# Differential attention: the fourth head through DRAM, norms by square transposes in tasks of their own, other banks for the values

## Chip, cores and metric

The kernel runs on one core of one Trainium2 chip. The metric is the device time of one execution in microseconds (us), the median of several runs. A core has a matrix engine (TensorE, PE), a vector engine (VectorE, DVE), a scalar engine (ScalarE, ACT), a general engine (GpSimd, POOL), a queue processor (SyncE, SP) and 16 DMA engines; each runs its own instruction stream in order and waits on semaphores.

## What is computed

One layer of a streaming encoder for 512 tokens of 1024 channels in float32: four mixers (A differential attention, B forgetting attention, C a convolution module, D a short gated convolution) fed by one input projection and merged by gates, then cross-attention into 256 memory tokens, then a gated MLP. The change touches branch A:

```python
s = einsum('bqhcd,bkhcd->bhcqk', q_blk, k) * scale          # 4 heads, 2 components c of 64 channels
mask = k_chunk[None, :] <= (tq_blk // CHUNK)[:, None]        # chunks of 64 tokens
p = softmax(where(mask, s, -inf), axis=-1)
a = p[:, :, 0] - lam * p[:, :, 1]
ya = einsum('bhqk,bkhe->bqhe', a, v)                         # e: 128 channels of a head
ya = rms_norm(ya, diff_norm) * (1 - lambda_init)             # over the 128 channels
```

## The kernel before

All matrix products are float32 work in reduced passes: an operand is split into a high part and a low remainder (ACT writes the high part, DVE subtracts it to get the low one), and three matmuls hi*hi, hi*lo, lo*hi are summed in a bank (`mm3`). Activations lie with channels on the partitions and tokens along the row (`ht`, high and low); weights stream in through SP, are split into `wh` and `wl`, and each block of weights is one job of `run_blocks`, which fetches three jobs ahead.

Beside the jobs runs a planner, `Background(0.7, 2)`. Attention heads and norms are Python generators ("tasks") that emit a few instructions at each step and yield a cost and a wait. A clock advances with every matmul and transpose emitted (0.00042 per column, 0.107 per turn); at each `tick`, after a job and in the middle of some, the first two tasks of the queue may take steps whose wait is over, as far as a credit of 0.7 per unit of clock allows. `drain(name)` steps the named tasks to their end without letting the clock decide. What is emitted is then ordered for each engine by a scheduler at build time, which works on its own estimates of durations and moves an instruction ahead of others when its inputs and buffers are free; `tc.issue_after` and `keep` restrict it. The order on each engine is fixed in the program.

`mixer_jobs` sets the order around the change: branch D's gates, A's value products, then for each of the four heads of A its query and key products (`qk_jobs`), which add `a_task`, and some of the twelve gate jobs of branch C (0, 2, 4, 6 after the four heads); then `drain("a")`, branch B's value products (`vf_jobs`; the code calls branch B "f" and its values "vf"), B's heads (`f_task`) beside branch A's gate jobs.

`a_task` for a head: for each of four blocks of 128 queries, scores of both components into two "sc" banks (the block sees 128, 256, 384 or 512 keys), mask and maximum by a DVE operation into an "e" tile, two exponentials on ACT, reciprocals, and the difference of the two scaled parts (line 943). The result has queries on the partitions, and the values need it with keys there. For heads 0 to 2 (`far`), this turn is done by DVE in squares of 32x32 (`turn_squares`, line 854), a store to DRAM (`put`, line 859) and a load that places the squares (`get`, line 866), then a split in place (lines 872 and 873), at steps of their own; 8 steps. For head 3 it is done by PE matmuls with an identity (`to_keys_major`, `transpose`, line 247); 6 steps. `values` multiplies by the head's values into one "av" bank for two blocks at a time; a copy (line 952) takes the bank to an e tile. The norm over the head's channels follows in the same task, for every head: four turns by the identity bring tokens to the partitions, ACT squares (line 958), DVE sums (line 960), POOL takes the power (line 286), DVE scales (line 962), four more turns bring the channels back, and a split writes `y["a"]` (lines 164 and 165).

Two resources matter. Of e tiles there are three (`bufs=3`), which blocks, copies and other tasks share. Of PSUM there are eight banks: two each of "mm", "av" and "sc", one "tr0" and one "tr1"; in this stage the gate and query products rotate over mm, mm, tr0, and turns use tr1. The values of A and of B each fill the one tile tagged "v" (`bufs=1`).

`vf_jobs` multiplies the tokens by B's value weights: first tokens blocks 0 and 1, each into an mm and an av bank (256 and 264 columns), then, after their evacuation (`done`), blocks 2 and 3 into mm and av again.

`over_channels` (line 877) is one matmul with a 128x128 matrix `across`, which adds up, for each of the 32 positions within a square, the four partition groups; the convolution's norm uses it with sums over 32x32 squares that `by_token` groups.

Of the kernel before, what the change touches and what calls it, by code (L numbers as in the profile page):

```python
# [25 lines left out]
P = 128  # L26
# [20 lines left out]
class Background:  # L47
# [7 lines left out]
        self.queue, self.rate, self.width = [], rate, width  # L55
        self.clock = self.last = self.credit = 0.0

    def add(self, gen, name):
        self.queue.append([name, gen, 0.0])

    def step(self, task):
        try:
# [7 lines left out]
    def tick(self):  # L70
        self.credit = min(self.credit + (self.clock - self.last) * self.rate, 4.0)
        self.last = self.clock
        for task in list(self.queue[:self.width]):
            while self.credit > 0 and task in self.queue and task[2] <= self.clock:
                self.credit -= self.step(task)

# [7 lines left out]
def hybrid_layer(ctx: ExitStack, tc: tile.TileContext, a: dict, out: bass.AP):  # L84
# [751 lines left out]
    def to_keys_major(e, n, pt, local):  # L836

        ps = bank("tr")
        for kt in range(n):
            transpose(ps[:, kt * P:(kt + 1) * P], e[:, kt * P:(kt + 1) * P])  # L840
        split(ps[:, :n * P].rearrange("p (t a i) -> p a t i", t=n, a=4), *(x[:, local, :, :n] for x in pt))
# [9 lines left out]
    def turn_squares(dst, src):  # L851
        if len(dst.shape) == 2:
            dst = dst.rearrange("p (b t i) -> p b t i", b=4, i=32)
        V.transpose(dst, src.rearrange("p (t j b) -> p b t j", b=4, j=32))
# [10 lines left out]
    def get(d, n, pt, local):  # L865
        SP.dma_start(part_of(pt[1], n, local).bitcast(F32), d.rearrange("(a j) (b x) -> (j b) a x", j=32, b=4))

    def split_in_place(n, pt, local):
        hi, lo = (part_of(x, n, local) for x in pt)
        raw = lo.bitcast(F32)  # L870
        with tc.issue_after(evacuations[0]):
            A.copy(hi, raw)
        V.tensor_tensor(lo, raw, hi.bitcast(F32), ALU.subtract)
# [21 lines left out]
    def pt_tiles():  # L895
        return tuple(m1p.tile([P, 2, 4, 4, 32], F32R, tag=n, name=n, bufs=2) for n in ("pth", "ptl"))
# [3 lines left out]

    def a_task(h, qk, v):
        es, pt, av = {}, None, None
        far = h < 3
        yield 0.0, 3.0
        for step in range(8 if far else 6):
            if step in ((5, 7) if far else (3, 5)):
                if av is None:
                    av = bank("av")
                vh, vl = (x[:, :, h * P:(h + 1) * P] for x in v[0])
                with tc.issue_after(steps_of[0]) if far else ExitStack():  # L910
                    values(av, lambda kt: ((vh[:, kt], 0), (vh[:, kt], 1), (vl[:, kt], 0)), pt,
                           step // 2 - (2 if far else 1))
            cost = 0.0
            if far:
                for qt in SPLITS.get(step, ()):
                    split_in_place(qt + 1, pt, qt % 2)
                    cost += 0.1 + 0.15 * qt
                for qt in GETS.get(step, ()):
                    if qt % 2 == 0:
                        pt = pt_tiles()  # L920
                    get(es.pop(qt)[:, 0], qt + 1, pt, qt % 2)
            elif 1 <= step <= 4:
                if step in (1, 3):
                    pt = pt_tiles()
                to_keys_major(es.pop(step - 1)[:, 0], step, pt, (step - 1) % 2)
                cost += 0.1 + 0.15 * step
            if step < 4:
                qt, w = step, (step + 1) * P
                e = es[qt] = e4()
                st = m1p.tile([P, 8], F32, tag="st8", name="st8", bufs=4)  # L930
                for c in range(2):
                    ps = bank("sc")
                    scores(ps, qk, c, qt * P, w)
                    V.tensor_tensor_reduce(e[:, c, :w], ps[:, :w], mask_a[:, S - w:], scale=-HD ** -0.5,
                                           scalar=3.0e38, op0=ALU.add, op1=ALU.min,
                                           accum_out=st[:, c:c + 1])
                for c in range(2):
                    A.activation(e[:, c, :w], e[:, c, :w], AF.Exp, bias=st[:, c:c + 1],
                                 scale=-1.0, accum_out=st[:, 4 + c:5 + c])
                V.reciprocal(st[:, 6:8], st[:, 4:6])  # L940
                V.tensor_scalar(st[:, 7:8], st[:, 7:8], lam, None, ALU.mult)
                A.activation(e[:, 1, :w], e[:, 1, :w], AF.Copy, scale=st[:, 7:8])
                V.scalar_tensor_tensor(e[:, 0, :w], e[:, 0, :w], st[:, 6:7], e[:, 1, :w], ALU.mult,
                                       ALU.subtract)
                cost += 0.6 + 0.0035 * w
                if far:
                    turn_squares(e[:, 1, :w], e[:, 0, :w])
                    es[qt] = put(e[:, 1:], w)
                    cost += 0.0015 * w
            if step == (7 if far else 5):  # L950
                e = e4()
                A.copy(e[:, 0], av)
            yield cost, (6.0 if step == 5 else 4.0) if far else 3.5

        ps = bank("tr")
        for t in range(NT):
            transpose(ps[:, t * P:(t + 1) * P], e[:, 0, t * P:(t + 1) * P])
        A.activation(e[:, 1], ps, AF.Square, scale=1.0 / math.sqrt(P))
        ms = m1p.tile([P, NT], F32, tag="ms4", name="ms4", bufs=2)
        V.tensor_reduce(ms, e[:, 1].rearrange("p (t c) -> p t c", t=NT), AX.X, ALU.add)  # L960
        r = rstd_of(m1p, [ms], NT)
        V.tensor_tensor(e[:, 0].rearrange("p (t c) -> p t c", t=NT),
                        ps.rearrange("p (t c) -> p t c", t=NT),
                        r.unsqueeze(2).to_broadcast([P, NT, P]), ALU.mult)
        yield 1.5, 3.5
        ps2 = bank("tr")
        for t in range(NT):
            transpose(ps2[:, t * P:(t + 1) * P], e[:, 0, t * P:(t + 1) * P])
        if "a" not in y:
            y["a"] = (y8b(), y8b())  # L970
        split(ps2, y["a"][0][:, h], y["a"][1][:, h], half["dn"])
        yield 0.6, 0.0


    crows = dram.tile([8, S], F32, name="crows")
# [2 lines left out]
    def vf_jobs(dst):  # L978

        ps, held = {}, []  # L980
        groups = ((0, 256), (256, 520))

        def products(kb, tokens):
            hi, lo = held[kb]
            for t in tokens:
                sl = slice(t * P, (t + 1) * P)
                for k in range(2):
                    kk = kb * 2 + k
                    for g, (c0, c1) in enumerate(groups):
                        mm3(ps[t, g][:, :c1 - c0], ht[0][:, kk, sl], ht[1][:, kk, sl], hi[:, k, c0:c1],  # L990
                            lo[:, k, c0:c1], kk == 0, kk == NK - 1)

        def done(t):
            for g in range(2):
                hs = slice(4 * g, 4 * g + 4)
                split(ps[t, g][:, :256].rearrange("p (h c) -> p h c", h=4), dst[0][:, t, hs, 0], dst[0][:, t, hs, 1])
            V.tensor_copy(dst[1][:, t], ps[t, 1][:, 256:264])

        for kb in range(4):
            def body(hi, lo, kb=kb):  # L1000
                held.append((hi, lo))
                if kb == 0:
                    dst.append(m1p.tile([P, NT, 8, 2, HD], F32R, tag="v", name="v"))
                    dst.append(small["fz_raw"].rearrange("p (t h) -> p t h", t=NT))
                    ps.update({(t, g): bank(("mm", "av")[g]) for t in range(2) for g in range(2)})
                products(kb, (0, 1))
                if kb < 3:
                    return
                done(0)
                done(1)  # L1010
                bg.tick()
                ps.update({(t, g): bank(("mm", "av")[g]) for t in range(2, 4) for g in range(2)})
                for b in range(4):
                    products(b, (2, 3))
                    bg.tick()
                done(2)
                done(3)
                forget_gates(dst[1])

            yield *cols(w_in, O_FV, BR + 8, kb * 2, 2), body  # L1020
# [181 lines left out]
    def mixer_jobs():  # L1202
# [20 lines left out]
        yield from vj  # L1223
        yield share("mm", "mm", "tr0")
        gc = gate_blocks(2, "c")
        for h, n in enumerate((0, 2, 4, 6)):
            yield from qk_jobs(O_AQ, O_AK, h, lambda qk, h=h: bg.add(a_task(h, qk, va), "a"))
            if n:
                yield then(lambda: bg.drain("conv"))
            for _ in range(n):  # L1230
                yield next(gc)
# [666 lines left out]
```

## Time and profile before

| | us |
|---|---|
| median of 3 runs (lowest to highest) | 1048.19 (1047.79 to 1048.29) |
| the profiled execution, its own time | 1047.26 |
| its span, first to last instruction | 1045.5 |
| busy TensorE / VectorE / ScalarE / GpSimd | 1035.8 / 809.6 / 510.6 / 143.3 |

All rows of the profile are from one execution. Times in it start at the first instruction. A row of a timeline reads: start, length, engine, line, operation, output tile <- input tiles, shapes, count, and in brackets the idle time before it with what ended it. "PE ps_mm" is a matmul that writes a bank tagged mm. Lengths of matmul records overlap, since matmuls are pipelined; the chain of work that ended last gives each piece the time that it adds. In the groups by line the columns are busy time and mean length, then the engine's idle time before the group and what ended it. A row of the waits names the waiting engine, tile and line, whom it waited for, the total, how often, and the longest.

### The profile page before, as it was taken

How to read it: one execution, taken by the hardware profiler on the slowest of the kernel's cores; microseconds unless marked ns; L12 is line 12 of the kernel's file. 1: busy time of each engine (PE TensorE's matmuls, PEld its weight loads, DVE VectorE, ACT ScalarE, POOL GpSimd, SP SyncE). 2: the span in 40 equal slices, each digit the busy share in tenths (PEclk: the TensorE clock that was granted, in tenths of full speed). 3: DMA queues.
4: the chain of work that ended last, by engine and by line, in shares of the span. 5: the costliest groups of instructions: out<-in, count | busy, mean ns of one | idle time of the engine just before them, and what ended most of it. 6: DMA issues, size and time to landing. Idle time of an engine off the chain costs nothing.

```text
span 1045.5 us, 14417 instructions
## 1 busy us (share of the span) xinstructions
PE 1035.8 (99%) x5235; PEld 880.7 (84%) x5235; DVE 809.6 (77%) x1241; ACT 510.6 (49%) x838; POOL 143.3 (14%) x239
## 2 busy tenths in 40 slices
PE   9999999999999999999999999999999999999997
PEld 8888888888888988888888899998888888888886
DVE  7999998677787367878577898777767777667786
ACT  5322222376565365666444566555343333445662
POOL 4001000100010123342101031121112111111001
PEclk9999999999999999999999999999999999999999
DMA  8954333334433246666338744135676676626662
GB/s 271 311 156 100 101 101 101 91 91 121 142 104 109 62 122 178 184 165 158 120 124 287 237 134 127 62 108 184 193 240 229 214 227 217 220 82 183 216 214 82
DMA packets 187453, 166.48 MB, mean 159 GB/s; under 512 B 20415, under 2 KB 159148, under 8 KB 187381
## 3 DMA queue, kind: packets, MB, share of 16 engines
q1 hardware_dynamic: 178339, 133.80, 43.1%
q10 hardware_dynamic: 6482, 23.21, 6.1%
q0 software_dynamic: 2560, 8.54, 2.7%
q8 instruction: 41, 0.67, 0.3%
q14 instruction: 31, 0.25, 0.1%
HBM read 140.74 MB, written 24.79 MB: 158 GB/s over the span
## 4 chain that ended last, share of the span: by engine, by line
PE 99%; DMA 0%; DVE 0%; issue 0%; POOL 0%; POOLq 0%; DVEq 0%; SPq 0%; ACT 0%; ACTq 0%
PE ps_mm L241 47%; PE ps_av L241 30%; PE ps_tr L241 11%; PE ps_sc L241 7%; PE ps_tr L247 2%; PE ps_mm L459 1%; PE ps_av L459 1%; DMA xs<-in_x 0%; PE ps_tr L443 0%; DVE o L1788 0%; PE ps_av L443 0%; DVE nt L438 0%; DVE ge L1183 0%; DVE nt L412 0%; POOL st_m L285 0%
## 5 line engine op out<-in xcount | busy, mean ns | idle before, releaser
L198 ACT CAST wh<-wr 128x1024 fp32r<-128x1024 f32 (+1 forms) x140 | 146.5, 1047 | 233.5 <-PE ps_mm L241 121.2
L199 DVE TENSOR_TENSOR wl<-wr,wh 128x1024 fp32r<-128x1024 f32 (+1 forms) x140 | 174.8, 1249 | 86.2 <-ACT wh L198 85.4
L241 PE MATMUL ps_mm<-hth,wh 128*128 128x512 f32 (+1 forms) x536 | 198.9, 378 | 0.0
L241 PE MATMUL ps_mm<-htl,wh 128*128 128x512 f32 (+1 forms) x536 | 198.3, 377 | 0.0
L241 PE MATMUL ps_mm<-hth,wl 128*128 128x512 f32 (+1 forms) x536 | 198.3, 377 | 0.0
L241 PE MATMUL ps_av<-hth,wh 128*128 128x512 f32 (+1 forms) x328 | 122.5, 374 | 0.0
L241 PE MATMUL ps_av<-htl,wh 128*128 128x512 f32 (+1 forms) x328 | 122.5, 373 | 0.0
L241 PE MATMUL ps_av<-hth,wl 128*128 128x512 f32 (+1 forms) x328 | 122.3, 373 | 0.0
L241 PEld LDWEIGHTS ps_mm<-hth,wl 128*128 128x128 f32 x536 | 99.0, 188 | 18.3
L241 PEld LDWEIGHTS ps_mm<-hth,wh 128*128 128x128 f32 x536 | 99.0, 188 | 17.9 <-ACT hth L161 0.3
L241 PEld LDWEIGHTS ps_mm<-htl,wh 128*128 128x128 f32 x536 | 98.9, 188 | 17.9
L694 DVE SCALAR_TENSOR_TENSOR y<-y,par,y 128x508 f32<-128x508 f32 (+29 forms) x120 | 82.5, 725 | 0.1
L241 PEld LDWEIGHTS ps_av<-hth,wh 128*128 128x128 f32 x328 | 61.6, 188 | 11.1 <-DVE e L1154 0.3
L241 PEld LDWEIGHTS ps_av<-htl,wh 128*128 128x128 f32 x328 | 61.6, 188 | 10.9
L241 PEld LDWEIGHTS ps_av<-hth,wl 128*128 128x128 f32 x328 | 61.6, 188 | 10.9
L1689 DVE TENSOR_TENSOR wl<-dw,wh 128x1024 fp32r<-128x1024 f32 x32 | 40.2, 1260 | 15.0 <-ACT wh L1688 14.7
L1688 ACT CAST wh<-dw 128x1024 fp32r<-128x1024 f32 x32 | 33.4, 1051 | 22.2 <-PE ps_mm L241 7.4
L1636 ACT ACTIVATE th<-c 128x512 f32<-128x512 f32 x22 | 13.9, 632 | 48.8 <-DVE c L621 48.8
L1123 POOL TENSOR_SCALAR fbias<-ck,cq 128x128 f32<-128x128 f32 (+3 forms) x32 | 23.4, 739 | 73.0 <-DVE st L1129 66.6
L621 DVE SCALAR_TENSOR_TENSOR c<-ps_mm,par,c 128x510 f32<-128x510 f32 (+1 forms) x44 | 32.7, 744 | 0.7
L241 PE MATMUL ps_tr<-hth,wh 128*128 128x512 f32 x80 | 31.8, 398 | 0.0
L241 PE MATMUL ps_tr<-htl,wh 128*128 128x512 f32 x80 | 31.6, 395 | 0.0
(503 smaller groups left out, 2227.9 us busy)
## 6 DMA issues: line engine op xcount, KB each, us to landing
wr<-in_w_up SPq DMA_DIRECT2D x44, 512.0 KB
wr<-in_w_in SPq DMA_DIRECT2D x38, 512.0 KB
wr<-in_w_gate SPq DMA_DIRECT2D x32, 512.0 KB
wp<-in_w_down ACTq DMA_DIRECT2D x22, 512.0 KB
sums<-wp ACTq DMA_DIRECT2D x22, 512.0 KB
dw<-sums SPq DMA_DIRECT2D x44, 256.0 KB
wr<-in_w_branch SPq DMA_DIRECT2D x16, 512.0 KB
wide<-in_w_out SPq DMA_DIRECT2D x12, 512.0 KB
```

What stands on the lines that cost most here:

```text
L198: last_weights[:] = [order(A.copy(hi, raw[:, :n])).ins, low.tensor_tensor(lo, raw[:, :n], hi.bitcast(F32), ALU.subtract).ins]
L199: low.tensor_tensor(lo, raw[:, :n], hi.bitcast(F32), ALU.subtract).ins]
L241: steps_of[:] = [PE.matmul(ps, lhs, rhs, start=start, stop=stop).ins]
L247: turns.append(PE.transpose(ps, x, ident[:n, :n]).ins)
L459: keep(PE.matmul(banks[c][:, :S // 2], w[p == 1][:, k, c * P:(c + 1) * P], ht[p == 2][:, i * 4 + k, :S // 2], start=(i, p, k) == (0, 0, 0) ...
L621: ins = V.scalar_tensor_tensor(dst[:, s:], src[:, :S - s], w(k), dst[:, s:], ALU.mult, ALU.add)
L694: ins = V.scalar_tensor_tensor(dst[:, s:], src[:, :S - s], pc("conv_dw", k * 4 + j), dst[:, s:], ALU.mult, ALU.add)
L1123: G.tensor_scalar(bias[:, :w], ck[j][:, :w], -1.0, cq[:, qt, head:head + 1], ALU.mult, ALU.add)
L1636: A.activation(th, c[:, 0], AF.Silu)
L1688: A.copy(hi, x)
L1689: V.tensor_tensor(lo, x, hi.bitcast(F32), ALU.subtract)
```

## The change

Head 3 now takes the same way as heads 0 to 2 (8 steps, through DRAM). The norm leaves `a_task` and becomes a task of its own, `head_norm`, which the planner puts at the head of its queue with a wait of 4.0 and steps beside the two others: tasks added with `beside` raise the number of tasks that a tick may step. The norm uses DVE's square transposes in place of turns by the identity: after one, sums over 32 of the channels lie along the row, `over_channels` adds the four partition groups, the power is taken for 16 columns, the scaled squares are turned back and split. No turn by the identity is left in branch A. The gate jobs of branch C are dealt out as 0, 2, 3, 7. `vf_jobs` uses mm and sc for blocks 0 and 1, and av, tr0, av, mm for blocks 2 and 3.

```diff
@@ class Background
+    def add(self, gen, name, beside=None):
+        if beside is None:
+            self.queue.append([name, gen, 0.0, 0])
+        else:
+            self.queue.insert(0, [name, gen, self.clock + beside, 1])
...
-        for task in list(self.queue[:self.width]):
+        for task in list(self.queue[:self.width + sum(t[3] for t in self.queue)]):
@@ a_task
-        far = h < 3
...
-        for step in range(8 if far else 6):
+        for step in range(8):
...
-                to_keys_major(es.pop(step - 1)[:, 0], step, pt, (step - 1) % 2)
...
+                turn_squares(e[:, 1, :w], e[:, 0, :w])
+                es[qt] = put(e[:, 1:], w)
...
+            yield cost, 6.0 if step == 5 else 4.0
+        bg.add(head_norm(h, e), "a", 4.0)
+
+    def head_norm(h, e):
+        V.transpose(e[:, 1], e[:, 0])
+        A.activation(e[:, 0], e[:, 1], AF.Square, scale=1.0 / math.sqrt(P))
+        ms = m1p.tile([P, S // 32], F32, tag="ms4", name="ms4")
+        V.tensor_reduce(ms, by_token(e[:, 0]), AX.X, ALU.add)
+        yield 1.0, 4.0
         ps = bank("tr")
-        for t in range(NT):
-            transpose(ps[:, t * P:(t + 1) * P], e[:, 0, t * P:(t + 1) * P])
...
+        over_channels(ps[:, :S // 32], ms)
+        V.tensor_scalar(ms, ps[:, :S // 32], EPS, None, ALU.add)
+        G.tensor_tensor(ms, ms, nhalf[:, :1].to_broadcast([P, S // 32]), ALU.pow)
+        yield 0.2, 4.0
+        V.tensor_tensor(by_token(e[:, 1]), by_token(e[:, 1]), ms.unsqueeze(2).to_broadcast([P, S // 32, 32]), ALU.mult)
+        V.transpose(e[:, 0], e[:, 1])
...
+        split(e[:, 0], y["a"][0][:, h], y["a"][1][:, h], half["dn"])
+        yield 1.0, 0.0
@@ vf_jobs
-                    ps.update({(t, g): bank(("mm", "av")[g]) for t in range(2) for g in range(2)})
+                    ps.update({(t, g): bank(("mm", "sc")[g]) for t in range(2) for g in range(2)})
...
-                ps.update({(t, g): bank(("mm", "av")[g]) for t in range(2, 4) for g in range(2)})
+                ps.update({(2 + i // 2, i % 2): bank(tag) for i, tag in enumerate(("av", "tr0", "av", "mm"))})
@@ mixer_jobs
-        for h, n in enumerate((0, 2, 4, 6)):
+        for h, n in enumerate((0, 2, 3, 7)):
```

More of the change, by code (lines that the diff above doesn't have):

```diff
@@ L56, in __init__ @@
         self.clock = self.last = self.credit = 0.0
-    def add(self, gen, name):
-        self.queue.append([name, gen, 0.0])
+    def add(self, gen, name, beside=None):
[3 more added lines that the diff above has]
+            self.queue.insert(0, [name, gen, self.clock + beside, 1])
     def step(self, task):
@@ L902, in a_task @@
         es, pt, av = {}, None, None
-        far = h < 3
         yield 0.0, 3.0
-        for step in range(8 if far else 6):
-            if step in ((5, 7) if far else (3, 5)):
+        for step in range(8):
+            if step in (5, 7):
                 if av is None:
@@ L909, in a_task @@
                 vh, vl = (x[:, :, h * P:(h + 1) * P] for x in v[0])
-                with tc.issue_after(steps_of[0]) if far else ExitStack():
+                with tc.issue_after(steps_of[0]):
                     values(av, lambda kt: ((vh[:, kt], 0), (vh[:, kt], 1), (vl[:, kt], 0)), pt,
-                           step // 2 - (2 if far else 1))
+                           step // 2 - 2)
             cost = 0.0
[L914 to L923, printed above, removed]
+            for qt in SPLITS.get(step, ()):
+                split_in_place(qt + 1, pt, qt % 2)
+                cost += 0.1 + 0.15 * qt
+            for qt in GETS.get(step, ()):
+                if qt % 2 == 0:
                     pt = pt_tiles()
-                to_keys_major(es.pop(step - 1)[:, 0], step, pt, (step - 1) % 2)
-                cost += 0.1 + 0.15 * step
+                get(es.pop(qt)[:, 0], qt + 1, pt, qt % 2)
             if step < 4:
@@ L944, in a_task @@
                                        ALU.subtract)
[L945 to L950, printed above, removed]
+                turn_squares(e[:, 1, :w], e[:, 0, :w])
+                es[qt] = put(e[:, 1:], w)
+                cost += 0.6 + 0.005 * w
+            if step == 7:
                 e = e4()
@@ L952, in a_task @@
                 A.copy(e[:, 0], av)
-            yield cost, (6.0 if step == 5 else 4.0) if far else 3.5
-        ps = bank("tr")
-        for t in range(NT):
-            transpose(ps[:, t * P:(t + 1) * P], e[:, 0, t * P:(t + 1) * P])
[L958 to L968, printed above, removed]
+            yield cost, 6.0 if step == 5 else 4.0
[6 more added lines that the diff above has]
+        yield 1.0, 4.0
+        ps = bank("tr")
+        over_channels(ps[:, :S // 32], ms)
[4 more added lines that the diff above has]
+        V.transpose(e[:, 0], e[:, 1])
@@ L969, in a_task @@
         if "a" not in y:
             y["a"] = (y8b(), y8b())
-        split(ps2, y["a"][0][:, h], y["a"][1][:, h], half["dn"])
-        yield 0.6, 0.0
+        split(e[:, 0], y["a"][0][:, h], y["a"][1][:, h], half["dn"])
+        yield 1.0, 0.0
     crows = dram.tile([8, S], F32, name="crows")
```

## The prediction

> **What bounds the kernel now.** I read the busy times first, then the chain of work that ended last, then what TensorE (PE) waits for. The first row is busy time by engine, the second the chain's shares, the other two the whole list of PE's waits:
>
> ```profile
> PE 1035.8 (99%) x5235; PEld 880.7 (84%) x5235; DVE 809.6 (77%) x1241; ACT 510.6 (49%) x838; POOL 143.3 (14%) x239
> PE 99%; DMA 0%; DVE 0%; issue 0%; POOL 0%; POOLq 0%; DVEq 0%; SPq 0%; ACT 0%; ACTq 0%
> PE ps_mm L400 <- DVE e L350: 1.3, 1, 1.3
> PE ps_tr L443 <- DVE nt L438: 1.2, 1, 1.2
> ```
>
> PE is the bound, and its only two waits lie in the start-up (lines 400 and 443), long before the change. So the time is the sum of what PE executes: whatever leaves its stream shortens the kernel by its spacing in the stream, and whatever makes PE wait lengthens it. Other engines count only where they are late for PE. The next view is busy time by stretch: columns are length, then PE, weight loads, DVE, ACT, POOL with instruction counts, clock, DMA share, GB/s. The first stretch is the differential attention beside gate blocks, the second the value products of branch B (`vf_jobs`):
>
> ```profile
> 228.00:338.00 110.00, 110.00 (x539) 92.57 (x538) 83.49 (x190) 68.42 (x145) 6.64 (x12) 1.00 0.41 118
> 338.00:366.00 28.00, 27.96 (x235) 27.68 (x234) 12.11 (x21) 9.78 (x19) 3.90 (x5) 1.00 0.22 58
> ```
>
> PE is full in both. VectorE (DVE) has 26.5 us idle in the first and 15.9 us in the second.
>
> **Turns taken off PE.** The change removes every turn by the identity that reads an attention tile here: 32 of the four heads' norms (8 each) and 10 of head 3's probabilities (1+2+3+4 blocks). The groups by line give their count, and the chain gives what each group takes of PE's stream:
>
> ```profile
> L247 PE MATMUL ps_tr<-ident,e 128*128 128x128 f32 x42 | 6.5, 272 | 0.0
> 284.63 0.44 PE ps_tr L247 x4
> 326.47 0.11 PE ps_tr L247
> 331.76 0.22 PE ps_tr L247 x2
> 339.12 0.35 PE ps_tr L247 x3
> 365.73 0.44 PE ps_tr L247 x4
> ```
>
> There are nine groups of four (the first and the last are shown), and one each of one, two and three: 9 x 0.44 + 0.11 + 0.22 + 0.35 = 4.64 us. The mean of 272 ns is the length of one record; the records overlap, so the chain's 0.11 us each is what leaves the stream. [...]
>
> **Work added on PE.** Each head gets one `over_channels`, the matmul by `across` on line 877 that the convolution's norm uses already. The timeline of PE around one, the chain's row for it, and the chain's row for a run of 512-column matmuls:
>
> ```profile
> 186.15 0.29 PE L877 MATMUL ps_tr<-bn,across 128*128 128x16 f32 x2
> 186.29 0.48 PE L241 MATMUL ps_mm<-y8b,wh 128*128 128x512 f32 x1
> 186.60 0.39 PE L241 MATMUL ps_mm<-y8b,wl 128*128 128x512 f32 x1
> 186.31 0.13 PE ps_tr L877 x2
> 46.00 5.44 PE ps_av L241 x24
> ```
>
> From 186.15 to 186.60 is 0.45 us for this and one 512-column matmul, whose own spacing is 0.23 us (5.44 us for 24). So it costs 0.22 us; the chain's 0.13 us is the other bound. Four times 0.22 is 0.88 us.
>
> Scores, values and gate products keep their number. The new order of gate blocks, (0,2,3,7) in place of (0,2,4,6), has twelve in both, so it costs PE nothing in itself.
>
> **Work added elsewhere, and its cover.** DVE's rows:
>
> ```profile
> L854 DVE STREAM_TRANSPOSE e<-e 128x128 f32<-128x128 f32 (+3 forms) x12 | 9.0, 753 | 0.2
> L165 DVE SCALAR_TENSOR_TENSOR y8b<-ps_tr,s_dn,y8b 128x512 fp32r<-128x512 f32 x2 | 1.5, 748 | 0.2 <-ACT y8b L164 0.2
> L962 DVE TENSOR_TENSOR e<-ps_tr,st_r 128x512 f32<-128x512 f32 x2 | 1.4, 690 | 1.5 <-POOL st_r L286 1.5
> L960 DVE TENSOR_REDUCE ms<-e 128x4 f32<-128x512 f32 x2 | 1.4, 676 | 0.0
> 198.75 0.17 DVE L711 TENSOR_SCALAR bn<-ps_tr 128x16 f32<-128x16 f32 x1 [0.51 <-PE ps_tr L877]
> 202.77 0.71 DVE L733 STREAM_TRANSPOSE xn<-y 128x512 f32<-128x512 f32 x1
> ```
>
> A head's norm is now a reduction, a product and a split, 0.68 + 0.69 + 0.75 = 2.12 us. It becomes two square transposes, reduction, small scalar, product and split: 1.42 + 0.68 + 0.17 + 0.69 + 0.75 = 3.71 us, so four heads add 6.4 us. Head 3 adds a far head's square transposes, 9.0 / 3 = 3.0 us; its splits only change their source. Some 9.4 us stand against 26.5 + 15.9 us of idle DVE: nothing on PE, and if the idle were not there, at most those 9.4 us. ACT's count hardly changes. POOL and SP's queue:
>
> ```profile
> 199.08 2.93 POOL L728 TENSOR_TENSOR bn<-bn,nhalf 128x16 f32<-128x16 f32 x1 [97.09 <-DVE bn L711]
> L808 POOL MEMSET qk<- 64x512 f32 x8 | 4.2, 520 | 71.1 <-PE ps_sc L241 47.4 <-DVE st L934 16.5 <-ACT y8b L164 7.0
> SPq L859 <- DVE e L854: 49.7, 17, 7.1
> ```
>
> POOL's power takes 2.93 us for 16 columns in place of a shorter one; behind it are queued the clearings of the next q tiles, which have 71 us of idle before them, so nothing. SP's queue gets four more stores and four more loads for head 3. Weight loads stand behind a store that waits for its square transpose (last row: up to 7.1 us now, over 17 waits). PE shows no wait for it, because weights come jobs ahead; I take 0, with 0 to 2 us as bounds.
>
> **Head 3's new path.** Its last query block must now go to DRAM and back before its last values, and branch B's values cannot be written until those are done, since both use the one tile tagged "v". Counting the planner's own clock by its code gives only an order: head 3's last scores come 14.0 units ahead of `vf_jobs` after, 11.7 before; at the drain its last two steps are issued without delay. The rows, with V the start of `vf_jobs` (338.0 in the windows):
>
> ```profile
> 318.82 1.08 DVE L854 STREAM_TRANSPOSE e<-e 128x512 f32<-128x512 f32 x1
> 339.12 0.75 DVE L943 SCALAR_TENSOR_TENSOR e<-e,st 128x512 f32<-128x512 f32 x1
> 279.65 0.33 SPq L859 DMA_DIRECT2D turned<-e  x1
> 281.19 2.43 SPq L866 DMA_DIRECT2D ptl<-turned  x2
> 286.86 0.62 ACT L872 CAST pth<-ptl 128x512 fp32r<-128x512 f32 x1
> 288.85 0.68 DVE L873 TENSOR_TENSOR ptl<-ptl,pth 128x512 fp32r<-128x512 f32 x1
> 348.01 1.25 PE ps_av L241 x11
> 349.29 0.59 ACT L952 COPY e<-ps_av 128x512 f32<-128x512 f32 x1 [0.65 <-PE ps_av L241]
> 364.07 0.35 PE ps_mm L241 x3
> 364.42 0.37 PE ps_av L241 x3
> ```
>
> Before, the block's last elementwise step ends at 339.87, V+1.9; 2.3 earlier is V-0.4. The square transpose (1.1) brings V+0.7. From head 1's store at 279.65 to its second load at 283.25 are 3.6 us, and to the first use at 286.86 as many again: V+7.9. Split 0.62 + 0.68, values 1.25, copy 0.59: V+11.0. Meanwhile PE has the 96 products of tokens 0 and 1, 0.12 us each by the last two rows, to V+11.5. The new banks add to that: scores' banks replace the av banks in the first half, and the first two banks of the second half (one av, tr0) need no values written, so 48 more products reach V+17.3. With the old banks the av pair would have been shared with head 3. So the slack is 6.3 us and the stall 0; its bounds, 0 and 6.7 us, are worked out with the rivals. The query product of branch B falls on tr0, now held by token 2; its evacuation lies beside token 3's products, so 0, and 1 us if it does not.
>
> **The sum.** -4.64 + 0.88 = -3.76 us. The profiled execution took 1047.26 us (span 1045.5 and 1.76 around it), so 1043.5; the median of the runs is 0.93 us higher, so the forecast is 1044.4 us. At 0.13 us per `over_channels` it would be 1044.1.
>
> **Rivals.** The rows that they use, of ACT, DVE and SP's queue:
>
> ```profile
> 285.50 0.51 ACT L872 CAST pth<-ptl 128x384 fp32r<-128x384 f32 x1 [5.31 <-DMA ptl<-turned]
> 310.58 0.69 DVE L934 CUSTOM_DVE_ANT_0 e<-ps_sc,mask_a 128x512 f32<-128x512 f32 x1 [1.20 <-PE ps_sc L241]
> 319.97 0.33 SPq L859 DMA_DIRECT2D turned<-e  x1
> ```
>
> First, the tail comes late by 8 to 12 us and PE idles for what exceeds 6.3: 1.7 to 5.9 us are given back, 1046.1 to 1050.3, about no change. For it: ACT waited 5.31 us for such a load, and at the drain no planned delay stands between load and use. Against it: PE waited for none of the twelve loads so far.
>
> Second, slower: the "e" tiles run out. There are three; a norm as a task of its own keeps one for some 25 units of the planner's clock against 13, and norms 0 and 1 overlap for ten, so one tile is left for heads 2 and 3. A 512-column block holds its tile from 310.58 to its store at 319.97 and 3.6 us on, 13 us. If head 3's last block is put off by one such residence, PE idles 13 - 6.3 = 6.7 us in `vf_jobs`: 1051.1. It decides for slower from 12.2 us of lateness. Against it: norms 0 and 1 are over before head 3's last block by the planner's clock.
>
> Third, the change saves more: if a turn took from PE the whole 272 ns of its record, 42 x 0.272 - 0.88 = 10.5 us would go, 1037.6. The spacing of 0.11 us leaves that almost no chance. [...] Fourth, the square transposes put the weight splits late and all of DVE's 9.4 us shows: 1053.8.
>
> **How the numbers follow.** Forecast 0.62; late tail 0.18; tiles 0.16; DVE 0.03; the dearer turn 0.01. The range goes from 1043.3 (the cheap `over_channels`, 0.5 us for the spread of the runs, and 0.3 us for a closer order of the small products) to 1050.3, the end of the late tail; outside lie the tiles, DVE and the dearer turn, 0.20. A measurement of this kernel can tell about 0.2%, 2.1 us, from no change: faster is below 1046.1, slower above 1050.3. So faster 0.63, same 0.18, slower 0.19.
>
> **What would show it.** Line 247's group on e tiles loses its 42, a matmul by `across` appears four times more, PE's list of waits stays empty past the start-up, and the stretch from the first head to the end of `vf_jobs` is 3.8 us shorter. A PE wait on ps_av in `vf_jobs` behind a load would show the late tail; one on scores, or DVE waits for a store before an e tile is written, the tiles. The forecast is wrong if PE waits for 1.7 us or more in all.

## The result, and the profile after

The changed kernel takes 1044.76 us (median of 7 runs, 1043.87 to 1045.38), the kernel before beside it 1047.79 us (7 runs, 1047.08 to 1049.58): ratio 0.997, 95% interval 0.996 to 0.9979. The forecast was 1044.4 us, the range 1043.3 to 1050.3. Two later comparisons of the same pair gave 1044.11 against 1047.46 (0.9965, 0.9952 to 0.9977) and 1043.69 against 1047.45 (0.9967, 0.9955 to 0.9979). The profiled execution took 1043.87 us, its span is 1042.1 us, 3.4 us less than before.

The page after, in the order of the prediction: busy times and the chain's shares.

```profile
PE 1032.0 (99%) x5201; PEld 877.1 (84%) x5201; DVE 816.3 (78%) x1257; ACT 511.0 (49%) x838; POOL 158.5 (15%) x235
PE 96%; DMA 2%; DVE 1%; ACT 0%; issue 0%; POOL 0%; POOLq 0%; DVEq 0%; SPq 0%; ACTq 0%
```

TensorE (PE) works 3.8 us less. VectorE works 6.7 us more and GpSimd 15.2 us more, and neither shows in the time. The chain now has 2% of DMA and 1% of VectorE, which were not there before. The list of PE's waits says why:

```profile
PE ps_mm L403 <- DVE e L353: 1.3, 1, 1.3
PE ps_tr L446 <- DVE nt L441: 1.0, 1, 1.0
PE ps_av L244 <- ACT pth L875: 0.7, 1, 0.7
```

The first two lie in the start-up as before. The third is new: PE waits once, 0.7 us, for the split of head 3's last probabilities. Next, the turns and what came for them, in the groups by line: the turns of e tiles before, the same group after, and the matmul by `across` on the norms' sums.

```profile
L247 PE MATMUL ps_tr<-ident,e 128*128 128x128 f32 (+1 forms) x66 | 10.3, 269 | 0.0
```
```profile
L250 PE MATMUL ps_tr<-ident,e 128*128 128x128 f32 (+1 forms) x24 | 3.8, 263 | 0.0
L880 PE MATMUL ps_tr<-ms,across 128*128 128x16 f32 x8 | 1.2, 220 | 0.0
```

The 42 turns are gone, and four `over_channels` (two records each) have come. Where the time went is seen in busy time by stretch. Both traces are divided at the first score product of branch A and at the last value product of branch B; each trace has two rows, first before, then after.

```profile
228.15:365.50 137.35, 137.31 (x766) 119.72 (x765) 95.05 (x207) 77.66 (x161) 10.54 (x17) 1.00 0.37 106
365.50:1045.50 680.00, 672.90 (x3379) 571.28 (x3376) 515.54 (x745) 349.82 (x566) 114.95 (x190) 1.00 0.56 173
```
```profile
228.07:362.57 134.50, 133.80 (x736) 116.72 (x735) 100.90 (x223) 77.12 (x160) 16.26 (x13) 1.00 0.40 112
362.57:1042.10 679.53, 672.42 (x3375) 570.84 (x3373) 516.32 (x744) 350.85 (x567) 124.47 (x191) 1.00 0.56 175
```

The changed stretch is 2.85 us shorter, with the 0.7 us wait inside. The rest is 0.47 us shorter: head 3's norm had four turns there (0.44 us in the prediction's chain row).

The end of head 3's new path, in the chain of waits of the changed kernel, and the first value product of branch B (V) and the wait in PE's timeline:

```profile
342.10 0.76 DVE e L939
342.89 1.10 DVE e L857
344.06 2.16 DMA turned<-e
346.24 3.66 DMA ptl<-turned
349.92 0.63 ACT pth L875
350.59 0.99 PE ps_av L244 x6
```
```profile
333.59 0.28 PE L244 MATMUL ps_tr<-wh,hth 128*128 128x264 f32 x1
350.59 0.39 PE L244 MATMUL ps_av<-pth,v 128*128 128x256 f32 x1 [0.70 <-ACT pth L875]
```

Read downwards, the chain is the step that the prediction had written out: last elementwise step (line 939), square transpose, store, load, split, values. The lengths are close to the forecast; the place is not. The elementwise step starts at V+8.5 and ends at V+9.3, where an end at V-0.4 was forecast. From V on PE had other products for 16.3 us (17.3 forecast), so it waited the last 0.7 us. The last row is one of head 3's value products and five of branch B's; head 3's values go on between branch B's products until 353.08, V+19.5.

### The profile page after: what moved, and what is told of

Read it like the earlier page. It is cut to its first block, busy times and chain, and to the rows that moved or that the text cites. A ratio compares the mean times of both kernels' runs of the same rounds, so it can differ in the third digit from the quotient of the medians.

```text
span 1042.1 us, 14386 instructions
## 1 busy us (share of the span) xinstructions
PE 1032.0 (99%) x5201; PEld 877.1 (84%) x5201; DVE 816.3 (78%) x1257; ACT 511.0 (49%) x838; POOL 158.5 (15%) x235
## 4 chain that ended last, share of the span: by engine, by line
PE 96%; DMA 2%; DVE 1%; ACT 0%; issue 0%; POOL 0%; POOLq 0%; DVEq 0%; SPq 0%; ACTq 0%
PE ps_mm L244 46%; PE ps_av L244 30%; PE ps_tr L244 11%; PE ps_sc L244 7%; PE ps_tr L250 1%; DMA ptl<-turned 1%; PE ps_mm L462 1%; PE ps_av L462 1%; DMA turned<-e 0%; DMA xs<-in_x 0%; DVE e L857 0%; DVE e L939 0%; PE ps_tr L446 0%; DVE wl L202 0%; DVE o L1782 0%
```

## Experiments

**What a turn takes.** The kernel before with the norms' turns issued twice:

```diff
         for t in range(NT):
             transpose(ps[:, t * P:(t + 1) * P], e[:, 0, t * P:(t + 1) * P])
+        for t in range(NT):
+            transpose(ps[:, t * P:(t + 1) * P], e[:, 0, t * P:(t + 1) * P])
...
         for t in range(NT):
             transpose(ps2[:, t * P:(t + 1) * P], e[:, 0, t * P:(t + 1) * P])
+        for t in range(NT):
+            transpose(ps2[:, t * P:(t + 1) * P], e[:, 0, t * P:(t + 1) * P])
```

> The kernel before, with each of the two groups of four turns by the identity in every head's norm issued twice (32 turns more, the second set writes the same values again). By the chain's spacing of 0.11 us a turn: +3.5 us against the kernel before. If a turn takes its record's 0.272 us from TensorE: +8.7 us. If turns lie beside other matmuls and take nothing: 0. The mean record length in the group stays near 270 ns in all three cases.

1050.57 us against 1047.44 us; ratio 1.003 (1.0019 to 1.0041). Its group of turns, and its stretch from the first score product to the end:

```profile
L247 PE MATMUL ps_tr<-ident,e 128*128 128x128 f32 (+1 forms) x98 | 13.9, 271 | 0.0
```
```profile
228.59:1049.40 820.81, 813.69 (x4175) 694.63 (x4173) 610.77 (x951) 426.84 (x726) 130.56 (x207) 1.00 0.52 161
```

The stretch was 137.35 + 680.00 = 817.35 us. 32 turns took 3.46 us in these two profiles, 0.108 us each, while a record is still 271 ns long. (The medians differ by 3.13 us, 0.098 us a turn.) The spacing is the price, not the record.

**One part alone: the norms.** The kernel before with `head_norm` and the planner's `beside`, and nothing else of the change:

```diff
-            transpose(ps[:, t * P:(t + 1) * P], e[:, 0, t * P:(t + 1) * P])
...
+        bg.add(head_norm(h, e), "a", 4.0)
```

> The kernel before with one part of the change: the norms of all four heads as tasks of their own by square transposes. Head 3 still turns its probabilities by the identity, the banks of branch B's values and the gate order are those of before. My sum: 32 turns at 0.11 us leave (-3.52 us), four over_channels at 0.22 us come (+0.88 us): -2.6 us against the kernel before, and no wait of TensorE in branch B's values. Rival, the detached norms hold e tiles and make head 3 late: head 3's last values come later against the first of branch B's value products than before, and TensorE waits there; each us of such a wait is taken off the gain. Rival, the over_channels costs only the chain's 0.13 us: -3.0 us.

1044.29 us against 1047.44 us; 0.9969 (0.9958 to 0.9981). Its stretches, divided at the same two products:

```profile
228.04:363.25 135.21, 134.95 (x746) 117.57 (x745) 98.36 (x217) 77.19 (x160) 17.97 (x13) 1.00 0.38 108
363.25:1042.80 679.55, 672.46 (x3375) 570.89 (x3373) 516.67 (x747) 350.25 (x567) 119.64 (x190) 1.00 0.56 173
```

Together 814.76 us, 2.59 us less than 817.35; the sum was 2.64. PE waits 0.3 us once, for a split of head 1. So the norms alone bring most of the gain; adding that wait back, 2.85 us left for 32 turns (3.46 us at 0.108), so one `over_channels` takes about 0.15 us, an estimate from the difference of two executions. The chain of the changed kernel gives the lower of my two bounds, 0.13 and 0.22 us; the row stands there three times between 284 and 372 us with this length:

```profile
289.23 0.13 PE ps_tr L880 x2
```

**The other part alone: head 3 through DRAM.** The changed kernel with the norm back in `a_task`, by turns with the identity:

```diff
-        bg.add(head_norm(h, e), "a", 4.0)
+            transpose(ps[:, t * P:(t + 1) * P], e[:, 0, t * P:(t + 1) * P])
```

> The changed kernel with the norms put back into the head's own task, by turns with the identity as before; head 3 still goes through DRAM, with the new banks and gate order. My sum: 10 turns at 0.11 us leave, -1.1 us against the kernel before, and norm 3's eight turns come in the stage after. If the lateness of head 3's last block in the changed kernel (its values could start 17 us after the first of branch B's value products, where I had forecast about 8) came from the detached norms that hold e tiles, head 3's last difference of probabilities lies back near the first of those products (-0.4 us forecast) and the 0.7 us wait of TensorE before its values is gone. If it came from the way through DRAM itself and the planner's order, the lateness stays at 8 to 9 us and the wait stays.

1047.7 us against 1047.44 us; 1.0002 (0.9993 to 1.001): no gain. Its stretches, its last elementwise step of head 3, and the two waits that it has in branch B's heads:

```profile
228.44:364.86 136.42, 136.42 (x760) 119.19 (x759) 97.41 (x213) 77.42 (x160) 9.51 (x17) 1.00 0.40 114
364.86:1045.80 680.94, 673.06 (x3375) 570.69 (x3373) 515.18 (x742) 350.71 (x567) 119.45 (x190) 1.00 0.56 173
```
```profile
342.31 0.75 DVE L939 SCALAR_TENSOR_TENSOR e<-e,st 128x512 f32<-128x512 f32 x1 [0.85 <-ACT e L938]
412.94 0.39 PE L244 MATMUL ps_av<-pth,v 128*128 128x256 f32 x1 [0.45 <-ACT pth L875]
446.73 0.39 PE L244 MATMUL ps_av<-ptl,v 128*128 128x256 f32 x1 [0.38 <-DVE ptl L876]
```

The ten turns are gained in the changed stretch (0.93 us of 1.10) and lost behind it (0.94 us, 0.83 of it in those waits). And the lateness is there without any norm as a task of its own: the last elementwise step is at 342.31 (its start), 6.9 us behind that kernel's V (335.41); in the changed kernel it is 8.5. My first explanation, that only the detached norms make head 3 late, falls. Of the rival, the lateness came, but not the wait: PE has no wait in this kernel's changed stretch.

**What the new banks are worth.** The changed kernel with `vf_jobs` as before:

```diff
-{(t, g): bank(("mm", "sc")[g]) for t in range(2) for g in range(2)}
+{(t, g): bank(("mm", "av")[g]) for t in range(2) for g in range(2)}
...
-enumerate(("av", "tr0", "av", "mm"))
+{(t, g): bank(("mm", "av")[g]) for t in range(2, 4) for g in range(2)}
```

> The changed kernel with the banks of branch B's values as before: mm and av for tokens 0 and 1 and again for 2 and 3. If the new banks are what covers head 3's way through DRAM, TensorE loses the 48 products (about 5.8 us at 0.12 us each) of tokens 2 and 3 that stand ahead of head 3's last values, and more if the av pair must be freed by head 3 first (up to 24 products more, 2.9 us): the wait before head 3's last values grows from 0.7 us to 6.5 to 9.4 us, and the time is 1050.5 to 1053.5 us. If the banks do not matter because the planner issues something else there: 1044.8 us, as the changed kernel.

1053.39 us against 1047.44 us; 1.0055 (1.0043 to 1.0068). So with this gate order the banks are what makes the change a gain. The time is at the end of the forecast, but not by the forecast wait: that was 5.7 us, below the 6.5 to 9.4 us expected. PE's longest wait, and busy time by stretch: the whole changed stretch, and the time at half clock.

```profile
PE ps_av L244 <- ACT pth L875: 5.7, 1, 5.7
```
```profile
228.48:373.09 144.61, 138.07 (x736) 120.50 (x735) 102.41 (x224) 77.96 (x160) 17.23 (x13) 0.96 0.39 110
351.10:361.33 10.23, 8.81 (x37) 8.33 (x38) 4.41 (x9) 3.26 (x7) 0.00 (x0) 0.50 0.01 2
```

The column before the last two is the granted clock: 0.50 for 10.23 us from 351.10, while PE was busy for 8.81 of them. Branch B's value products stand 0.22 us apart there and 0.12 us ahead of the wait; by the clock half of the 8.81, some 4.4 us, is lost on top of the wait, an estimate.

**What makes head 3 late.** Two edits beside the changed kernel itself and a fourth kernel, on one chip. First, the norms of heads 0 to 2 in two tiles that are idle in this stage:

```diff
-                e = e4()
-                A.copy(e[:, 0], av)
+                if h < 3:
+                    e = [m1p.tile([P, S], F32, tag="ck", name="ck", bufs=2) for _ in range(2)]
+                else:
+                    e = e4()
+                    e = [e[:, 0], e[:, 1]]
+                A.copy(e[0], av)
```

> The changed kernel once more, beside the kernels of this group on one chip: 1044.8 us, 3.0 us less than the kernel before, TensorE waits 0.7 us for head 3's last values. It is the measure for the three others.

> The changed kernel with the norms of heads 0 to 2 in two tiles tagged ck (free in this stage) instead of an e tile; only head 3's norm, the last, takes an e tile. If the norms' hold on the three e tiles is what puts head 3's last scores late (in the changed kernel 1.3 us behind the first of branch B's value products), they come about 4 us ahead of it, TensorE's 0.7 us wait before head 3's last values is gone and the time is 0.7 us below the changed kernel on this chip. Rival: the lateness is the way through DRAM itself. ScalarE, which works in order, waits 1.83 and 1.88 us for loads of head 3's own blocks while its next exponentials stand behind; the e tiles change nothing then, last scores and wait stay, 0.0 us.

Second, the old gate order, and third, the old gate order with the old banks:

```diff
-        for h, n in enumerate((0, 2, 3, 7)):
+        for h, n in enumerate((0, 2, 4, 6)):
```

> The changed kernel with the gate jobs dealt out as 0, 2, 4, 6 as before. My prediction: the order of the gates costs TensorE nothing, so the time of the changed kernel, 0.0 us. Rival: one more gate job (5.4 us of TensorE) ahead of heads 2 and 3 lets norm 1 end, and with it its e tile come free, before head 2's last block asks for it; then head 3's last scores come about 4 us ahead of the first of branch B's value products, the 0.7 us wait is gone and the time is 0.7 us below.

> The changed kernel with both the banks and the gate order of before. With the old banks and the new gate order TensorE waited 5.7 us for head 3's last values, and its granted clock stood at 0.50 for some 10 us behind the wait, which added about 4 us more than the wait. If the old gate order brings head 3's last scores some 4 us forward, the wait here is 1.5 to 2.5 us. If the clock falls only after a long wait, the time is the changed kernel's plus 1 to 2 us, 1045.8 to 1046.8 us; if a wait of this length is enough for the clock to fall, 1050 us. If the gate order does not matter, it is 1053.4 us again.

Measured: the changed kernel 1044.11 us, with ck tiles 1046.69 us (0.9991, 0.9983 to 1.0 against the 1047.46 us of before), with gates 0, 2, 4, 6 1045.26 us (0.9982, 0.9973 to 0.9991), with old gates and banks 1047.42 us (0.9998, 0.999 to 1.0007). VectorE's first operation on the scores of head 3's last block and its last elementwise step on it, in the changed kernel and with ck tiles; then the first of these with the old gates:

```profile
336.36 0.69 DVE L930 CUSTOM_DVE_ANT_0 e<-ps_sc,mask_a 128x512 f32<-128x512 f32 x1
...
341.89 0.75 DVE L939 SCALAR_TENSOR_TENSOR e<-e,st 128x512 f32<-128x512 f32 x1 [0.26 <-ACT e L938]
```
```profile
331.88 0.69 DVE L930 CUSTOM_DVE_ANT_0 e<-ps_sc,mask_a 128x512 f32<-128x512 f32 x1
...
338.52 0.74 DVE L939 SCALAR_TENSOR_TENSOR e<-e,st 128x512 f32<-128x512 f32 x1
```
```profile
330.56 0.68 DVE L930 CUSTOM_DVE_ANT_0 e<-ps_sc,mask_a 128x512 f32<-128x512 f32 x1
```

The first operation comes 4.5 and 5.8 us earlier, and neither kernel has a wait before head 3's last values. With ck tiles nothing but the tiles was changed, and the last step comes 3.4 us earlier; against V it starts at 4.1 us where the changed kernel has 8.1. So the norms' hold on the three e tiles (in a task of their own or not) is shown to account for some 4 of the 9.3 us of lateness; and the gate order, which I had priced at nothing, moves head 3 by as much. It shows as order and not as a wait: in the traces of these three kernels VectorE waits for no store between 228 and 345 us. So the hold acts, as far as the traces say, when the program is built and its order chosen. What makes up the rest of the lateness is not shown. Yet both kernels are slower than the changed one. The stretches with ck tiles, then with the old gates:

```profile
227.98:361.62 133.64, 133.64 (x736) 116.76 (x735) 100.66 (x221) 75.88 (x158) 18.00 (x13) 1.00 0.42 118
361.62:1046.20 684.58, 674.56 (x3375) 570.25 (x3373) 515.79 (x747) 349.73 (x569) 123.85 (x190) 1.00 0.55 172
```
```profile
228.00:361.60 133.60, 133.60 (x736) 116.66 (x735) 100.78 (x221) 77.13 (x158) 17.08 (x13) 1.00 0.41 119
361.60:1043.30 681.70, 673.83 (x3375) 570.53 (x3373) 515.68 (x746) 350.11 (x569) 120.19 (x190) 1.00 0.56 173
```

The changed stretch is as short as promised, 133.6 us, 3.7 us below before. What is lost lies behind it: 684.58 and 681.70 us where the changed kernel's first profile has 679.53. The fourth kernel, with old gates and old banks, has waits of 0.34 and 0.68 us in the changed stretch, shorter than the 1.5 to 2.5 us that I expected, its clock stays at 1.00, and it loses as much behind (681.86 us), so that its time lies above the 1045.8 to 1046.8 us expected. With the old gates, too, the new banks bring 2.2 us (1047.42 to 1045.26); with the new gates it was 9. The stall that I wanted to save was 0.7 us at most, and the second profile of the changed kernel does not have it at all; it has another one instead, in the merge (its stretches, the waits of PE, and what ScalarE waited for there):

```profile
228.24:361.81 133.57, 133.57 (x736) 116.71 (x735) 100.97 (x223) 77.13 (x160) 16.27 (x13) 1.00 0.40 113
361.81:1043.50 681.69, 672.62 (x3374) 570.62 (x3373) 516.70 (x744) 350.55 (x567) 120.29 (x191) 1.00 0.56 174
```
```profile
PE ps_mm L244 <- DVE ge L1177: 1.9, 1, 1.9
```
```profile
563.42 1.05 ACT L1310 CAST mth<-mn 128x1024 fp32r<-128x1024 f32 x1 [6.42 <-DMA mn<-turned_m]
```

This is a program that did not change between the two profiles. ScalarE waited for this load through DRAM, 200 us behind the change, in both: 5.73 us in the first, where the load came in time for PE, and 6.42 us here, where it did not. So one profile's 681.69 us says little against 679.53, and the old gates' 681.70 us has to be read by its kind: it has no such wait in the merge, and its median on this chip is 1.15 us above the changed kernel's. A wait of 1.9 us is about what the five runs of the changed kernel there spread by (1043.07 to 1045.25 us); that it is the cause of the spread is not shown.

**Is the loss behind a matter of order, and what does a middling wait cost?** The gate order 0, 2, 5, 5 brings head 3 forward and leaves PE's order in branch B's heads nearly as it is in the changed kernel; with the old banks it gives a wait between 0.7 and 5.7 us. The edits are the tuple of gates, and the banks as above.

> The changed kernel with the gate jobs dealt out as 0, 2, 5, 5. With 0, 2, 4, 6 head 3's last scores came earlier and the stretch from the first head to the end of branch B's value products was 3.75 us shorter than before (2.85 in the changed kernel's first profile, with its 0.7 us wait), but branch B's heads behind it got waits of their own and gave back 1.5 us. If those new waits come from the order of instructions that the build happened to choose for branch B's heads, and not from head 3 being earlier, a dealing that brings head 3 forward and leaves the later order nearly as it is in the changed kernel keeps the whole gain: no wait before head 3's last values, that stretch 3.7 us shorter than before, branch B's stage as in the changed kernel, 0.5 to 1 us below it where its 0.7 us wait shows, some 1043.5 us. Rival: whatever brings head 3 forward costs branch B's heads the same; then 1045.2 us, as with 0, 2, 4, 6.

> The changed kernel with the banks of before and the gate jobs as 0, 2, 5, 5. With the old banks and 0, 2, 3, 7 TensorE waited 5.7 us before head 3's last values and its clock was 0.50 for 10.2 us; with 0, 2, 4, 6 it waited 0.3 and 0.7 us and the clock stayed at 1.00. Here the order puts about 2.6 us more of TensorE's work ahead of those values than with 0, 2, 3, 7, so a wait of 2 to 4 us. [...]

> The changed kernel, beside the two others on one chip: 1044.1 to 1044.8 us.

The changed kernel 1043.69 us, gates 0, 2, 5, 5 1045.95 us (0.9983, 0.9974 to 0.9992 against 1047.45 us), these gates with the old banks 1050.89 us (1.0032, 1.0019 to 1.0044). The stretches of the first two:

```profile
228.17:361.97 133.80, 133.78 (x736) 116.71 (x735) 100.78 (x223) 77.13 (x160) 16.26 (x13) 1.00 0.40 112
361.97:1041.40 679.43, 672.29 (x3375) 570.73 (x3373) 517.00 (x744) 350.83 (x567) 119.31 (x191) 1.00 0.56 175
```
```profile
228.26:361.81 133.55, 133.55 (x736) 116.66 (x735) 100.98 (x223) 77.09 (x160) 16.39 (x13) 1.00 0.39 113
361.81:1044.50 682.69, 674.42 (x3375) 570.38 (x3373) 516.73 (x744) 350.81 (x567) 125.45 (x191) 1.00 0.56 174
```

Nearly the same order on PE, and a loss of some 3 us behind is there again: PE's order in branch B's heads is not its cause. The rival holds in kind; the time is 0.7 us above its 1045.2 us. Matched product by product, PE falls behind the changed kernel by 2.0 us in branch B's heads; the rest comes in the merge and at the end. ScalarE's timeline shows where it begins, at the first load of branch B's first head; the changed kernel, then gates 0, 2, 5, 5:

```profile
401.80 0.53 ACT L875 CAST pth<-ptl 128x128 fp32r<-128x128 f32 x2 [2.90 <-DMA ptl<-turned]
```
```profile
403.87 0.62 ACT L875 CAST pth<-ptl 128x128 fp32r<-128x128 f32 x2 [5.13 <-DMA ptl<-turned]
```

The split comes 2.1 us later (2.2 counted from the end of each changed stretch), everything of that head queues behind it on ScalarE, and PE waits or runs its small products further apart. The traces say where most of it comes from. The store ahead of this load is issued at the same time (394.83 and 394.89 us), but the load behind it, which waits for the store, at 398.76 and 400.17 us. With gates 0, 2, 5, 5 the DMA engines also carry a 16 KB packet of instructions during the store, from 397.40 to 398.34 us (its row in the DMA view of 397.3 to 398.4 us), and the store's last packets trail until 399.62 us:

```profile
q8 instruction: 1, 0.02, 5.3%
```

In the changed kernel that packet is over at 395.81 us and the store at 398.23. With gates 0, 2, 4, 6 it is as with 0, 2, 5, 5: the packet at 397.44 to 398.42 us, 5.2 us from store to load, where the three profiles of the changed kernel have 3.6 to 3.9. That the packet delays the store is read from these traces; no run moves the packet alone. It does not explain the kernel with ck tiles, whose store takes 3.6 us; what that one loses stays open.

The kernel with the middling wait: PE's waits in its timeline, and the whole changed stretch and the half clock.

```profile
348.14 0.39 PE L244 MATMUL ps_av<-pth,v 128*128 128x256 f32 x1 [2.53 <-ACT pth L875]
348.87 0.39 PE L244 MATMUL ps_av<-ptl,v 128*128 128x256 f32 x1 [0.34 <-DVE ptl L876]
351.06 0.59 PE L244 MATMUL ps_av<-wh,hth 128*128 128x264 f32 x1 [0.68 <-ACT e L946]
```
```profile
228.06:368.68 140.62, 137.07 (x736) 119.55 (x735) 102.89 (x224) 78.25 (x162) 17.07 (x13) 0.98 0.40 113
350.37:357.20 6.83, 6.16 (x29) 6.15 (x29) 3.01 (x8) 2.37 (x6) 0.00 (x0) 0.50 0.01 2
```

The wait of 2.53 us is within the 2 to 4 us expected. Behind it the clock is 0.50 for 6.83 us, where the wait of 5.71 us had 10.23. The stretch is 7.1 us longer than the 133.55 us of the same gates with the new banks: 3.5 us of waits, 3.1 us for the work at the clock of 0.50 (an estimate, half of 6.16), and 0.5 us that I do not attribute. So these waits cost about twice their length. With this gate order the new banks bring 4.9 us (1050.89 to 1045.95).

## Why the prediction was right, point by point

- **PE bounds, the rest is cover.** Right. The time followed PE's spacing; VectorE's added 6.7 us (9.4 forecast) and GpSimd's power (GpSimd is busy for 15.2 us more) cost nothing that a run showed. The range for SP's queue, 0 to 2 us, ended at 0: no wait of PE for weights came.
- **Turns, 42 x 0.11 = 4.64 us.** Right: 0.108 us each. The dearer turn is excluded.
- **`over_channels`, 0.22 us (0.13 to 0.22).** 0.13 in the chain of the changed kernel, about 0.15 by the norms alone: the lower bound was nearer, the 0.22 of the forecast too high.
- **The sum, -3.76 us.** The part that it adds up was worth a little more: with 0.13 us for each `over_channels` the same sum is -4.12 us. In the two profiles of the changed kernel without head 3's wait, the changed stretch is 133.57 and 133.80 us, 3.78 and 3.55 us below before; with the 0.47 us behind it 4.0 to 4.3 us. I had allowed 0.3 us for a closer order of small products; nothing in the runs asks for it. One of the signs did not fit the sum: the stretch to the end of `vf_jobs` was to be 3.8 us shorter, but four of the turns in the 4.64 us (0.44 us) lie behind it. The medians show 3.0, 3.4 and 3.8 us; in the first two profiles head 3's wait or the merge's takes part of the gain.
- **Head 3's new path: stall 0, slack 6.3 us.** The stall was right by luck. The way from store to use was right (344.06 to 349.92 is 5.9 us, 7.2 forecast). The cover was nearly right, 16.3 us for 17.3, and came from the banks, but not as counted: only 108 of the 144 products of branch B stand in it, and products of head 3 itself fill most of the rest. The place was wrong: the last elementwise step ended at V+9.3 instead of V-0.4. I had carried it over from the kernel before, where head 3 turned by the identity. Through DRAM its blocks keep an e tile until the store has landed, and the norms keep others. So the first of head 3's last values could start at V+17.0, where the forecast rows give V+8.5 (V+7.9 and the split of 0.62). The slack was not 6.3 us either: I had counted it to the copy behind the values, but what PE asks for is the first value product, so it was 16.3 - 8.5 = 7.8 us. A lateness of 8.5 us met a slack of 7.8: a wait of 0.7 us in one profile and none in two.
- **The rival of e tiles** had the mechanism in part right (some 4 of the 9.3 us), but as an order that the build chose: its sign, VectorE waiting for a store, is absent. Its size of 13 us was too large.
- **The late tail** came, by the lateness that I had given it: the copy behind head 3's last values ended at 353.70, V+20.1, 9.1 us behind the V+11.0 forecast and within its 8 to 12 us. The price that I gave it, 1.7 to 5.9 us, did not come, since the slack was larger and PE's order sets products of branch B between head 3's values. For a longer stall the price would have been too low: I priced a stall at its length, and in the two runs with waits of 2.53 and 5.71 us the stretch grew by 7.1 and 11.0 us.
- **Gate order "costs PE nothing in itself".** True of its products, wrong as a whole: in the changed kernel 0, 2, 4, 6 and 0, 2, 5, 5 change what waits behind and cost 1.2 and 2.3 us.
- **What is worth what.** The norms by themselves bring nearly the whole gain (1044.29 us, beside 1044.76, 1044.11 and 1043.69 of the whole change; the two were not run side by side, and the runs do not tell them apart). Head 3 through DRAM by itself brings none. Without the new banks it costs more than the norms bring with gates 0, 2, 3, 7 and 0, 2, 5, 5, and takes back all of it with 0, 2, 4, 6.

## What to carry to other kernels

Where one engine is the bound, price what you take off it by the spacing of its records (here 0.108 us a turn, where a record is 0.271 us long), and what you add to a side path by the slack that is left in the place where the main engine next asks for it; a place carried over from the old kernel is not that slack. When a path gets longer, give the main engine work that doesn't depend on it, here two banks; that decided 2, 5 and 9 us, by the gate order, where the removed work was 4. In a program with a fixed order, a small saving at one place can turn into small waits at the next tight place, so compare by stretches up to fixed products, not only by the end.

## What the runs showed of the hardware

The granted clock was 0.50 in two kernels, both with the old banks. With gates 0, 2, 3, 7 it was 0.50 for 10.23 us, beside a wait of 5.71 us; with gates 0, 2, 5, 5 for 6.83 us, behind a wait of 2.53 us (one of 0.34 us is close to it). In both, branch B's value products stand 0.12 us apart ahead of the wait and 0.22 us apart at the clock of 0.50, and behind it the clock was 1.00 again.

| old banks, gates | stretch, us | PE busy | granted clock |
|---|---|---|---|
| 0, 2, 3, 7 | 351.10 to 361.33 | 8.81 of 10.23 | 0.50 |
| 0, 2, 3, 7 | 361.33 to 373.09 | 11.76 of 11.76 | 1.00 |
| 0, 2, 5, 5 | 350.37 to 357.20 | 6.16 of 6.83 | 0.50 |
| 0, 2, 5, 5 | 357.20 to 360.60 | 3.40 of 3.40 | 1.00 |

In the stretches with waits of 0.70 us, of 0.34 and 0.68 us, and of 1.9 us (134.50, 135.14 and 681.69 us long) the mean clock was 1.00. In the last a fall of a few us would not show in the mean; the products of 512 columns there stand 0.23 us apart ahead of the wait and in the 2.4 us behind it. What decides when the clock falls and when it returns is not shown. In the two runs at 0.50 the stretch grew by 1.7 and 2.0 times the waits in it (11.0 us for 6.39, 7.1 us for 3.55).
